# A two-block hybrid network on one core: linear-attention decays laid out by key and query, five early up/gate tiles, first loads on two queues

## The chip, the cores and the metric

The kernel runs on one NeuronCore of a Trainium2 chip as one launch. The metric is device time in microseconds, the median of several executions. Lower is better. The engines that matter here are TensorE (PE; PEld is its weight load), VectorE (DVE), ScalarE (ACT), GpSimd (POOL) and SyncE (SP), which issues the loads.

## The reference

The input is x with 256 tokens of width 1024. Two networks run one after the other, each with two layers. A layer is a feed-forward stage, a mixer, and a second feed-forward stage; so there are eight feed-forward stages and four mixers.

```
def hybrid_layer(x, ...):                       # first network, twice
    x = x + 0.5 * swiglu(rmsnorm(x, ffn1_norm), wg, wu, wd)      # 1024 -> 2816 -> 1024
    h = rmsnorm(x, mix_norm); proj = h @ w_in
    na_o  = rmsnorm(neighbourhood_attention(na_q, na_k, na_v, rpb), na_gain)     # 8 heads of 64
    o_fwd = gla_chunked(qg, kg, vg, log_gf, True)                # 4 heads, dk 64, dv 128
    o_bwd = flip(gla_chunked(flip(qg), flip(kg), flip(vg), flip(log_gb), False))
    gla_o = rmsnorm(o_fwd + o_bwd, gla_gain) * silu(g_r)
    x = x + concat([na_o, gla_o]) @ w_out
    return x + 0.5 * swiglu(rmsnorm(x, ffn2_norm), ...)

def gla_chunked(q, k, v, g, include_diag):      # gated linear attention, one direction
    b = cumsum(g)
    a[t, s] = sum_d q[t, d] * k[s, d] * exp(b[t, d] - b[s, d])   # s <= t, or s < t
    o[t] = sum_s a[t, s] * v[s]                 # the state between chunks continues the same sum
```

The second network's feed-forward stages are the same with a shift, a scale and a gate that come from a vector c (modulation: c times nine matrices of 1024 x 1024 a layer); its mixers are a recurrent unit with block attention, and a sparse attention.

## The kernel before

**Layout.** x lies transposed in SBUF, as eight tiles of 128 features by 256 tokens (`k.x`). A matmul takes a 128x128 block of weights as the stationary operand and 256 tokens as the moving one. All weights are fp32; each is split into a high part (`wh`, fp32r, made on ScalarE, L319) and the rest (`wl`, made on VectorE, L332), and so are the activations.

**The weight stream** (`Stream`, L257 to L362). The weights are a list of chunks of 1 MB, 16 blocks of 128x128 each. A chunk is loaded on SyncE's queue into `stg` (L308), split, and used by TensorE in order. `AHEAD` chunks are split before TensorE uses them. Among the chunks of the first feed-forward stages stand pieces of the modulation matrices, which VectorE multiplies with c and sums (L701).

**The start** (`begin`, L271). The first chunk and x come in four pieces each; both were issued in turn on SyncE's queue (L283, L284). ScalarE and VectorE split each piece as it lands, and the first matmuls follow.

**A feed-forward stage** (`ffn`). It has 22 up/gate tiles. A tile is one chunk: eight blocks for gate, eight for up, 256 tokens, into one PSUM tile (`pp`, two of them). The RMS norm is not waited for. Tiles below `OLD` (0, 1 and 2) use the split of the unnormalised x times the norm's gain (`Hh`, `Hl`) with three matmuls a block (`mm3`, L622 to L624: wh Hh, wh Hl, wl Hh), and the row factor `rs` is multiplied in afterwards (L750). Here this is called the early form. During tile 1 the row factor is made (`norm_sum`, `norm_spread`), and then a background generator, `renorm` (L577), makes the normalised and split H, eight feature tiles one by one: a product on VectorE or GpSimd (L584), a copy to fp32r on ScalarE, the rest on VectorE (L687 without a shift, L684 with one). Tiles from `OLD` on read H with two matmuls a block (`mm2`, L606 of 512 columns, that is low and high part of H side by side, and L607 of 256). Then the down projection (`pd`) follows from `act`.

**Background work.** `tick()` is called after every few blocks of a tile; each call advances every generator in `self.bg` by one step, to its next `yield`. What a step issues is queued on the engines behind what was issued before; on TensorE the order is the order of issue. In a feed-forward tile there are four steps, in a q/k tile of mix1 two, in the last value projection of mix1 one after each 128 rows of weights.

**mix1** (two stages, at about 204 to 335 us and 704 to 840 us). Generators run beside the projections: `na_pair` for each pair of attention heads, and `gla_grams`, then `gla_out`, for the linear attention. `gla_grams` builds the 256 x 256 matrix a (keys by queries) for four heads and both directions in levels: blocks of 8, then pairs of half-blocks of 8, 16, 32 and 64, then the two halves of 128. INC is the running sum of the log gates, VAL the same shifted for the backward direction. For a level, `dist` makes the differences to the block's middle on VectorE (L941, L942) and their exponential on ScalarE (L943); `weigh` multiplies with q or k (L947, L948); `gram` is eight products on TensorE (16 matmul instructions, fp32, 64 partitions each, L955) into two PSUM tiles; `place` copies them under a mask into `at` (L965). The first index of the tensors was the direction, so each level had a Gram group for each direction. The order is one step `weigh`, one step the forward group, and so on, set by the `yield`s and `wait`s.

Of the kernel before, what the change touches and what calls it, by code (L numbers as in the profile page):

```python
# [17 lines left out]
P = 128  # L18
# [97 lines left out]
def gla_masks():  # L116

    s, t = np.arange(P)[:, None], np.arange(P)[None]
    m = [(s // 8 == t // 8) & (s > t)]
    for h in LEVELS:  # L120
        same = s // (2 * h) == t // (2 * h)
        left, right = s % (2 * h) < h, t % (2 * h) >= h
        m += [same & left & right, same & ~left & ~right]
    return np.ascontiguousarray(np.stack(m, 1).astype(np.uint8)).reshape(P, -1).view(np.int32)


# [130 lines left out]
class Stream:  # L257
# [13 lines left out]
    def begin(self, x, start, split):  # L271

        k, nc = self.k, self.k.nc
        t = k.wp.tile([P, CH * P], F32, name="stg", tag="stg")
        h = k.hp.tile([P, CH * P], F32R, name="wh", tag="wh", bufs=self.AHEAD + 2)
        l = k.hp.tile([P, CH * P], F32R, name="wl", tag="wl")
        parts = [slice(a, b) for a, b in PIECES]

        def part(w, m):
            return w.rearrange("p (g k n) -> p g k n", g=2, n=P)[:, :, m]  # L280

        for m in parts:
            nc.sync.dma_start(k.x[:, m], x[:, m])  # L283
            nc.sync.dma_start(part(t, m), part(self.plan[0][1], m))  # L284
        nc.sync.dma_start(k.ident, k.a["ident"])
        self.loaded = 1
        start()
        for m in parts:
            split(m.start)
            nc.scalar.activation(part(h, m), part(t, m), AF.Copy)  # L290
            nc.vector.tensor_sub(part(l, m), part(t, m), f(part(h, m)))
            for i in range(m.start + 1, m.stop):
                split(i)
        self.high = self.ready = 1
        self.parts[0] = (h, l)
        self.split_hi()
        self.prep()
# [68 lines left out]
SUM_ONE = 0, 7  # L366
SUM_TWO = 1, 7

OLD = 3

PIECES = (0, 2), (2, 4), (4, 6), (6, 8)

# [6 lines left out]
class Kern:  # L379
    def __init__(self, ctx, nc, tc, a, o):  # L380
        self.ctx, self.nc, self.tc, self.a, self.o = ctx, nc, tc, a, o
        self.wp = ctx.enter_context(tc.tile_pool(name="wp", bufs=Stream.LOADS))
        self.hp = ctx.enter_context(tc.tile_pool(name="hp", bufs=Stream.AHEAD + 1))
        self.cp = ctx.enter_context(tc.tile_pool(name="cp", bufs=1))
        self.tp = ctx.enter_context(tc.tile_pool(name="tp", bufs=2))
        self.pd = ctx.enter_context(tc.tile_pool(name="pd", bufs=2, space=PSUM))
        cp, nc = self.cp, self.nc
        self.x = cp.tile([P, KD, S], F32, name="x")
        self.Hh = cp.tile([P, KD, S + 2], F32R, name="Hh")
        self.Hl = cp.tile([P, KD, S], F32R, name="Hl")  # L390
# [6 lines left out]
        nc.scalar.activation(self.mhalf, self.ones[:, :8], AF.Copy, scale=-0.5)  # L397
# [179 lines left out]
    def renorm(self, pool, tp):  # L577
# [4 lines left out]
        for i in range(KD):  # L582
            y = tp.tile([P, S], F32, name="y", tag="y", bufs=3)
            (nc.gpsimd if i % 2 else nc.vector).tensor_tensor(y, x[:, i], rs, op=OP.mult)  # L584
            lo, hi = self.H[:, i, 0], self.H[:, i, 1]
            if shift is None:
                self.split(hi, lo, y, g[:, i:i + 1])
            else:
                h = tp.tile([P, S], F32, name="h", tag="h", bufs=2)
                nc.scalar.activation(h, y, AF.Identity, scale=g[:, i:i + 1], bias=shift[:, i:i + 1])  # L590
                self.split(hi, lo, h)
            if i % 2:
                yield
# [202 lines left out]
    def mix1(self, st, l, then):  # L796
        nc = self.nc
        with self.tc.tile_pool(name="mx", bufs=1) as mp, self.tc.tile_pool(name="m2", bufs=2) as m2, \
# [5 lines left out]
            wgate = mp.tile([64, S], F32, name="wgate")  # L804
            nc.gpsimd.memset(code, 1.0)
            nc.sync.dma_start(wgate, self.a[f"wgate_{l}"])
            qkq = mp.tile([P, 3, 2, S], F32, name="qkq")
            vg = mp.tile([P, 2, 512], F32, name="vg")
            vn = mp.tile([P, 2, 512], F32, name="vn")
            self.na = mp.tile([P, 4, S], F32, name="na")  # L810
# [21 lines left out]
                self.small()  # L832
            for i in range(2):
                p = self.tiles(st)
                nc.vector.scalar_tensor_tensor(qkq[:, 0, i], p[:, 0], 0.125, self.rs, op0=OP.mult, op1=OP.mult)
                nc.vector.tensor_mul(qkq[:, 1, i], p[:, 1], self.rs)
                nc.scalar.activation(qkq[:, 2, i], qkq[:, 0, i], AF.Copy)
            while gates in self.bg:
                self.tick()
            at = self.mp.tile([P, GH, 4, P], F32, name="at")  # L840

            def gla():
                yield from self.gla_grams(qkq, at)
                yield
                yield from self.gla_out(l, at, vg, sgr)

# [78 lines left out]
    def gla_grams(self, qkq, at):  # L925
        nc, mp, m2 = self.nc, self.mp, self.m2
        packed = mp.tile([P, (1 + 2 * len(LEVELS)) * P // 4], mybir.dt.int32, name="masks")
# [7 lines left out]
        def ref(h):  # L935
            r = INC.rearrange("p a i (n two h) -> p (a i n) two h", two=2, h=h)[:, :, 0, h - 1:h]
            return r.to_broadcast([P, 1024 // (2 * h), h])
# [12 lines left out]
        def gram(ks, qs, d, so=(0, P), to=(0, P)):  # L950

            ps = [self.pd.tile([P, 2, 2, P], F32, name="pg", tag="pd") for _ in range(2)]
            for i, j, hh in [(i, j, hh) for i in range(2) for j in range(2) for hh in range(2)]:
                r = slice(64 * hh, 64 * hh + 64)
                nc.tensor.matmul(ps[hh][:, i, j], ks[r, d[j], i, so[j]:so[j] + P], qs[r, d[j], i, to[j]:to[j] + P],  # L955
                                 start=True, stop=True)
            return ps

        def place(ps, m):
# [6 lines left out]


        d8 = m2.tile([P, 2, 2, S], F32, name="d8", tag="E")
        XR = mp.tile([P, 2, 2, S], F32, name="XR", tag="az")
        XL = mp.tile([P, 2, 2, S], F32, name="XL", tag="G")  # L970
# [6 lines left out]
        nc.vector.tensor_mul(XR, XR, qkq[:, 0:2])  # L977
        nc.vector.tensor_mul(XL, XL, qkq[:, 1:3])
        yield from wait(3)
        weigh(E, LEVELS[0])  # L980
        todo = (gram(XL, XR, (0, 0)), None)
        yield from wait(2)
        place(*todo)
        todo = (gram(XR, XL, (1, 1)), 0)
        yield from wait(2)
        hs = LEVELS + (128,)
        for n, h in enumerate(LEVELS):
            nxt = hs[n + 1]
            place(*todo)
            E2 = dist(nxt)  # L990
            todo = (gram(E, E, (0, 0)), 1 + 2 * n)
            yield from wait(2)
            place(*todo)
            weigh(E2, nxt)
            todo = (gram(E, E, (1, 1)), 2 + 2 * n)
            E = E2
            yield from wait(2 if n < 2 else 1)
        place(*todo)
        todo = gram(E, E, (0, 1), (0, P), (P, 0))
# [685 lines left out]
```

## Time and profile before

| | |
|---|---|
| median of 3 runs | 2029.94 us (2028.47 to 2030.31) |
| the profiled execution | 2029.0 us, span 2027.2 us |
| mean granted TensorE clock | 0.995 |
| PE busy | 1980.2 us, 98% |
| DVE busy | 1608.9 us, 79% |
| ACT busy | 1188.2 us, 59% |
| HBM read | 427.86 MB, 212 GB/s over the span |

The profile is one execution. Times in it count from the first instruction. An engine's busy share is an average over stages; what a stage waits for is read from the idle time ahead of its instructions and from what ended it (behind the arrow). A clock of 1.00 is 2.4 GHz, 0.50 is 1.2 GHz.

### The profile page before, as it was taken

The page shows a single profiled execution, that of the slowest core. Times are in us where ns is not written, and L with a number is a line of the kernel's source. Part 1 is how long each engine was busy: PE and PEld are TensorE (multiplying, and loading weights), DVE is VectorE, ACT ScalarE, POOL GpSimd, SP SyncE. Part 2 cuts the span into 40 slices and gives each one's busy share as a digit, 9 for nine tenths or more (in the row PEclk, how much of TensorE's full clock was granted, in tenths as well). Part 3 has the DMA queues.
Part 4 walks back from the last instruction along what each step waited for, and adds up shares of the span by engine and source line. Part 5 has one row for each costly group of instructions (what it writes and reads, how often), then busy time and mean ns, then how long its engine had stood idle before and what let it go on. Part 6 is the DMA issues. An engine that isn't in the chain of part 4 may idle for free.

```text
span 2027.2 us, 32869 instructions
## 1 busy us (share of the span) xinstructions
PE 1980.2 (98%) x13012; PEld 1778.4 (88%) x13012; DVE 1608.9 (79%) x2562; ACT 1188.2 (59%) x1990; POOL 181.0 (9%) x200
## 2 busy tenths in 40 slices
PE   7999999999999999999999999999999999999998
PEld 6888989888888898988888889888898888878887
DVE  8886797987888689798878877898667667978663
ACT  6654656554555465665555547575546555877552
POOL 2001002000100100200120010120010001101001
PEclk9999999999999999999999999999999999999999
DMA  7776434877588643487758765358555556315551
GB/s 283 292 282 247 164 143 157 292 271 288 211 287 294 234 158 140 157 307 275 268 184 293 284 246 185 125 218 290 188 189 185 187 189 201 121 43 188 189 188 60
DMA packets 67882, 431.03 MB, mean 213 GB/s; under 512 B 11408, under 2 KB 14096, under 8 KB 16656
## 3 DMA queue, kind: packets, MB, share of 16 engines
q1 hardware_dynamic: 67728, 428.94, 58.8%
q8 instruction: 102, 1.67, 0.3%
q14 instruction: 52, 0.43, 0.1%
HBM read 427.86 MB, written 1.05 MB: 212 GB/s over the span
## 4 chain that ended last, share of the span: by engine, by line
PE 82%; DVE 10%; ACT 4%; DMA 2%; issue 1%; POOL 0%; SPq 0%; DVEq 0%; ACTq 0%; POOLq 0%
PE pp L606 27%; PE pd L606 16%; PE pp L607 14%; PE pd L607 8%; DVE wl L332 3%; PE pp L622 2%; PE pp L623 2%; PE pp L624 2%; PE po L885 2%; ACT wh L319 1%; PE pt L1277 1%; PE pg L955 1%; DVE t L750 1%; DVE H L687 1%; PE pv L672 1%
## 5 line engine op out<-in xcount | busy, mean ns | idle before, releaser
L332 DVE TENSOR_TENSOR wl<-stg,wh 128x1024 fp32r<-128x1024 f32 x646 | 788.3, 1247 | 124.9 <-PE pp L607 57.3
L606 PE MATMUL pp<-H,wh 128*128 128x512 f32 x2432 | 849.6, 392 | 15.8 <-DVE H L687 7.9
L319 ACT ACTIVATE wh<-stg 128x1024 fp32r<-128x1024 f32 x646 | 668.3, 1053 | 327.2 <-PE pp L606 145.8
L607 PE MATMUL pp<-H,wl 128*128 128x256 f32 x2432 | 686.9, 283 | 0.0
L606 PEld LDWEIGHTS pp<-H,wh 128*128 128x128 f32 x2432 | 458.3, 189 | 115.7 <-DVE H L687 9.5
L606 PE MATMUL pd<-act,wh 128*128 128x512 f32 x1408 | 488.5, 390 | 0.0
L607 PEld LDWEIGHTS pp<-H,wl 128*128 128x128 f32 x2432 | 461.6, 190 | 0.3
L607 PE MATMUL pd<-act,wl 128*128 128x256 f32 x1408 | 397.1, 282 | 0.0
L606 PEld LDWEIGHTS pd<-act,wh 128*128 128x128 f32 x1408 | 264.3, 188 | 55.4
L622 PE MATMUL pp<-Hh,wh 128*128 128x258 f32 (+1 forms) x936 | 271.9, 291 | 7.0 <-ACT wh L290 6.3
L624 PE MATMUL pp<-Hh,wl 128*128 128x258 f32 (+1 forms) x936 | 264.7, 283 | 2.1 <-DVE wl L332 1.2
L607 PEld LDWEIGHTS pd<-act,wl 128*128 128x128 f32 x1408 | 266.1, 189 | 0.0
L623 PE MATMUL pp<-Hl,wh 128*128 128x256 f32 x936 | 264.2, 282 | 1.9 <-DVE Hl L687 1.9
L701 DVE SCALAR_TENSOR_TENSOR stg<-stg,cond 128x1024 f32<-128x1024 f32 x144 | 175.7, 1222 | 29.8 <-DMA stg<-mw 27.3
L622 PEld LDWEIGHTS pp<-Hh,wh 128*128 128x128 f32 x936 | 177.2, 189 | 11.8 <-ACT wh L290 6.3
L623 PEld LDWEIGHTS pp<-Hl,wh 128*128 128x128 f32 x936 | 178.4, 191 | 3.7 <-DVE Hl L687 2.5
L624 PEld LDWEIGHTS pp<-Hh,wl 128*128 128x128 f32 x936 | 177.4, 190 | 3.0 <-DVE wl L332 1.6
L683 ACT ACTIVATE act<-a 128x256 fp32r<-128x256 f32 x176 | 73.3, 417 | 128.5 <-DVE a L759 126.3
L522 POOL TENSOR_TENSOR acc<-sq 128x256 f32<-128x256 f32 x16 | 17.8, 1113 | 1204.5 <-ACT sq L518 1129.6
L684 DVE TENSOR_TENSOR act<-a,act 128x256 fp32r<-128x256 f32 x176 | 76.4, 434 | 45.9 <-ACT act L683 45.9
L522 POOL TENSOR_TENSOR acc<-acc,sq 128x256 f32<-128x256 f32 x87 | 78.6, 906 | 333.8 <-ACT sq L518 329.6
L615 DVE TENSOR_TENSOR t<-pp,c 128x512 f32<-128x512 f32 x152 | 104.0, 684 | 2.4 <-ACT c L613 2.4
(316 smaller groups left out, 2086.0 us busy)
## 6 DMA issues: line engine op xcount, KB each, us to landing
stg<-b SPq DMA_DIRECT2D x132, 1024.0 KB, 4.8
stg<-a SPq DMA_DIRECT2D x129, 1024.0 KB, 4.8
stg<-mw SPq DMA_DIRECT2D x72, 1024.0 KB, 5.2
stg<-m SPq DMA_DIRECT2D x34, 1024.0 KB, 4.8
stg<-m2a SPq DMA_DIRECT2D x14, 1024.0 KB, 4.8
stg<-m2b SPq DMA_DIRECT2D x12, 1024.0 KB, 4.8
stg<-nab SPq DMA_DIRECT2D x4, 1024.0 KB, 4.7
cond<-cond SPq DMA_DIRECT2D x6, 512.0 KB, 4.0
```

The source lines that it names most:

```text
L319: self.k.nc.scalar.activation(h[:, sl], self.raw[c][:, sl], AF.Copy)
L332: self.k.nc.vector.tensor_sub(l[:, sl], t[:, sl], f(h[:, sl]))
L522: nc.gpsimd.tensor_tensor(s2, acc, sq, op=OP.add)
L606: mm(p, h, parts, start=start, stop=False)
L607: return mm(p[:, :S], l, parts[:, 1], start=False, stop=stop)
L615: self.nc.vector.tensor_tensor(t, p[:, :, S:], c, op=OP.add)
L622: mm(out[:, :n], h, self.Hh[:, kt, :n], start=start and clear, stop=False, skip_group_check=not clear)
L623: mm(out[:, :S], h, self.Hl[:, kt], start=False, stop=False, skip_group_check=not clear)
L624: return mm(out[:, :n], l, self.Hh[:, kt, :n], start=False, stop=stop, skip_group_check=not clear)
L683: nc.scalar.activation(hi, src, AF.Copy)
L684: nc.vector.tensor_sub(lo, src, f(hi))
L701: self.nc.vector.scalar_tensor_tensor(sl, sl, 1.0, self.cond, op0=OP.mult, op1=OP.mult, accum_out=self.mod[l][:, 2 * c + g:2 * c + g + 1])
```

## The change

Four edits in one. `gla_grams` lays the decayed tensors out by key (0) and query (1) in place of direction; in a level the left half of a block belongs to the forward direction for keys and to the backward one for queries, so one Gram group and one mask give both. Its waits are set anew: three steps a level. `OLD` goes from 3 to 5, and `renorm` yields after each feature tile in place of every second. The first two x pieces are issued on ScalarE's queue, and the small constant `mhalf` is made behind them. `na_pair` takes the PSUM tile of a head and issues both products of this head before the next head's.

```
 def gla_masks():
-        m += [same & left & right, same & ~left & ~right]
+        m.append(same & (left == right))
 def begin():
-        for m in parts:
-            nc.sync.dma_start(k.x[:, m], x[:, m])
+        for n, m in enumerate(parts):
+            (nc.scalar if n < 2 else nc.sync).dma_start(k.x[:, m], x[:, m])
             nc.sync.dma_start(part(t, m), part(self.plan[0][1], m))
+        nc.scalar.activation(k.mhalf, k.ones[:, :8], AF.Copy, scale=-0.5)      # was in __init__
-OLD = 3
+OLD = 5
 def renorm():
-            if i % 2:
-                yield
+            yield
 def mix1():
-            qkq = mp.tile([P, 3, 2, S], F32, name="qkq")
+            kq = mp.tile([P, 2, 2, S], F32, name="kq")
-                nc.vector.scalar_tensor_tensor(qkq[:, 0, i], p[:, 0], 0.125, self.rs, op0=OP.mult, op1=OP.mult)
-                nc.vector.tensor_mul(qkq[:, 1, i], p[:, 1], self.rs)
-                nc.scalar.activation(qkq[:, 2, i], qkq[:, 0, i], AF.Copy)
+                nc.vector.scalar_tensor_tensor(kq[:, 1, i], p[:, 0], 0.125, self.rs, op0=OP.mult, op1=OP.mult)
+                nc.vector.tensor_mul(kq[:, 0, i], p[:, 1], self.rs)
 def gla_grams():
         def dist(h):
-            nc.vector.tensor_sub(cut(E, h, 1), cut(VAL, h, 1), ref(h))
-            nc.vector.tensor_sub(cut(E, h, 0), ref(h), cut(VAL, h, 0))
+            for d in range(2):
+                nc.vector.tensor_sub(cut(E[:, 1 - d:2 - d], h, 1), cut(VAL[:, d:d + 1], h, 1), ref(INC[:, d:d + 1], h))
+            nc.vector.tensor_sub(cut(E, h, 0), ref(INC, h), cut(VAL, h, 0))
             nc.scalar.activation(E, E, AF.Exp, scale=1.0 / 16)
-        def weigh(E, h):
-            nc.vector.tensor_mul(cut(E, h, 1), cut(E, h, 1), cut(qkq[:, 0:2], h, 1))
-            nc.vector.tensor_mul(cut(E, h, 0), cut(E, h, 0), cut(qkq[:, 1:3], h, 0))
+        def weigh(E):
+            nc.vector.tensor_mul(E, E, kq)
...
-        nc.scalar.activation(XR, d8, AF.Exp, scale=1.0 / 16)
-        nc.scalar.activation(XL, d8, AF.Exp, scale=-1.0 / 16)
+        for d in range(2):
+            for a in range(2):
+                nc.scalar.activation(X[d][:, a], d8[:, d], AF.Exp, scale=(-1.0 if a == d else 1.0) / 16)
...
-        for n, h in enumerate(LEVELS):
-            nxt = hs[n + 1]
+        for n in range(len(LEVELS)):
             place(*todo)
-            E2 = dist(nxt)
-            todo = (gram(E, E, (0, 0)), 1 + 2 * n)
+            E2 = dist(hs[n + 1])
+            todo = (gram(E[:, 0], E[:, 1]), 1 + n)
             yield from wait(2)
-            place(*todo)
-            weigh(E2, nxt)
-            todo = (gram(E, E, (1, 1)), 2 + 2 * n)
+            weigh(E2)
             E = E2
-            yield from wait(2 if n < 2 else 1)
+            yield
 def na_pair():
-        ss = [self.ps.tile([P, 2, S], F32, name="pss", tag="st", bufs=self.nst) for _ in range(2)]
-        for qt in range(2):
-            for hh, p in enumerate(ss):
-                r = slice(64 * hh, 64 * hh + 64)
+        ss = []
+        for hh in range(2):
+            r = slice(64 * hh, 64 * hh + 64)
+            p = self.ps.tile([P, 2, S], F32, name="pss", tag="st", bufs=self.nst)
+            for qt in range(2):
                 nc.tensor.matmul(p[:, qt], qk[r, 0, qt * P:(qt + 1) * P], qk[r, 1], start=True, stop=True)
+            ss.append(p)
```

## Rows read from the trace of the kernel before

**Rows 1.** The page, part 1: busy us, share of the span, instructions.

```profile
PE 1980.2 (98%) x13012; PEld 1778.4 (88%) x13012; DVE 1608.9 (79%) x2562; ACT 1188.2 (59%) x1990; POOL 181.0 (9%) x200
```

**Rows 2.** Groups by line and form: busy us, mean ns, idle us before, releasers.

```profile
L606 PE MATMUL pp<-H,wh 128*128 128x512 f32 x2432 | 849.6, 392 | 15.8 <-DVE H L687 7.9 <-DVE H L684 6.3 <-DVE b L693 1.7
```

**Rows 3.** Stretches of tile 3, line 606: length, busy (count), clock, DMA; eight summed.

```profile
29.01:41.58 12.57, 8.39 (x17) 4.26 (x17) 0.73 0.55 204
...
1047.09:1058.27 11.18, 7.35 (x16) 3.72 (x17) 0.85 0.26 95
...
sum 67.79, PE 50.40 PEld 25.92; mean PE 6.30 PEld 3.24
```

**Rows 4.** Stretches of tile 8, line 606: the sum of eight stages.

```profile
sum 44.39, PE 44.39 PEld 24.04; mean PE 5.55 PEld 3.00
```

**Rows 5.** Stretches: PE, PEld, DVE, ACT, POOL busy, granted clock, DMA share, GB/s.

```profile
33.83:40.66 6.83, 5.97 (x18) 5.09 (x19) 6.83 (x14) 3.90 (x7) 0.90 (x1) 0.50 0.49 170
279.59:283.00 3.41, 3.41 (x13) 2.59 (x14) 3.41 (x6) 0.79 (x2) 0.00 (x0) 0.50 0.00 0
1054.41:1057.83 3.42, 3.42 (x13) 2.84 (x12) 2.87 (x4) 0.42 (x1) 0.00 (x0) 0.50 0.00 0
```

**Rows 6.** Stretches of tile 2, line 622: the first and the sum of eight.

```profile
23.36:29.01 5.65, 4.47 (x16) 2.89 (x16) 1.00 0.70 271
...
sum 45.53, PE 36.00 PEld 23.13; mean PE 4.50 PEld 2.89
```

**Rows 7.** A stretch, columns as in rows 5, while tile 3 of the first stage waits.

```profile
30.00:36.00 6.00, 2.16 (x8) 1.41 (x7) 6.00 (x11) 3.65 (x7) 1.99 (x2) 0.82 0.71 276
```

**Rows 8.** Timeline of DVE, first feed-forward stage: start us, us, instruction.

```profile
36.03 0.47 DVE L687 SCALAR_TENSOR_TENSOR H<-y,cols,H 128x256 fp32r<-128x256 f32 x1
...
39.05 1.21 DVE L332 TENSOR_TENSOR wl<-stg,wh 128x1024 fp32r<-128x1024 f32 x1
...
40.52 1.21 DVE L332 TENSOR_TENSOR wl<-stg,wh 128x1024 fp32r<-128x1024 f32 x1
```

**Rows 9.** Groups by line and form, as in rows 2.

```profile
L332 DVE TENSOR_TENSOR wl<-stg,wh 128x1024 fp32r<-128x1024 f32 x646 | 788.3, 1247 | 124.9 <-PE pp L607 57.3 <-PE pd L607 45.2 <-issue 11.6
...
L759 DVE TENSOR_TENSOR a<-s,t 128x256 f32<-128x256 f32 x164 | 69.1, 421 | 32.1 <-ACT s L746 31.7 <-ACT s L753 0.3
...
L965 DVE COPY_PREDICATED at<-masks,pg 128x512 f32<-128x512 uint8 x36 | 24.4, 729 | 2.8 <-PE pg L955 2.8
...
L750 DVE TENSOR_TENSOR t<-pp,rs 128x512 f32<-128x512 f32 x24 | 16.4, 683 | 7.5 <-ACT rs L569 6.5 <-PE pp L624 0.9
...
L943 ACT ACTIVATE E<-E 128x1024 f32<-128x1024 f32 x10 | 10.5, 1052 | 10.6 <-DVE E L942 10.6
```

**Rows 10.** Timeline of PE in the first mix1: start us, us, instruction.

```profile
269.45 1.13 PE L1057 MATMUL pss<-qk 64*128 64x256 f32 x8
...
274.24 1.16 PE L955 MATMUL pg<-E 64*128 64x128 f32 x16
275.33 1.08 PE L1091 MATMUL pav<-pt,vn 128*64 128x256 f32 x8
...
277.86 0.67 PE L1057 MATMUL pss<-qk 64*128 64x256 f32 x2 [0.42 <-DVE qk L856]
279.47 1.99 PE L1057 MATMUL pss<-qk 64*128 64x256 f32 x6 [0.95 <-ACT sq L518]
...
304.91 1.89 PE L1017 MATMUL pgo<-at,vg 128*128 128x256 f32 x8
```

**Rows 11.** Timeline of SP, the first and the last issue of x.

```profile
1.18 0.42 SPq L283 DMA_DIRECT2D x<-xT  x1
...
4.84 0.60 SPq L283 DMA_DIRECT2D x<-xT  x1
```

**Rows 12.** The chain that ended last, the first tile: start us, us, what.

```profile
4.84 5.72 DMA x<-xT
```

**Rows 13.** A stretch, columns as in rows 5: the first pieces land.

```profile
6.30:13.20 6.90, 5.94 (x25) 5.51 (x26) 6.90 (x10) 5.11 (x11) 4.49 (x6) 1.00 0.97 340
```

More of the change, by code (lines that the diff above doesn't have):

```diff
@@ L396, in __init__ @@
         nc.gpsimd.memset(self.ones, 1.0)
-        nc.scalar.activation(self.mhalf, self.ones[:, :8], AF.Copy, scale=-0.5)
         nc.sync.dma_start(self.cols[:, :KD], a["cols"][:, :KD])
@@ L842, in gla @@
             def gla():
-                yield from self.gla_grams(qkq, at)
+                yield from self.gla_grams(kq, at)
                 yield
@@ L923, in gla_gates, with gla_grams @@
         nc.scalar.activation(self.VAL[:, 0], self.INC[:, 0], AF.Copy)
-    def gla_grams(self, qkq, at):
+    def gla_grams(self, kq, at):
         nc, mp, m2 = self.nc, self.mp, self.m2
-        packed = mp.tile([P, (1 + 2 * len(LEVELS)) * P // 4], mybir.dt.int32, name="masks")
+        packed = mp.tile([P, (1 + len(LEVELS)) * P // 4], mybir.dt.int32, name="masks")
         nc.sync.dma_start(packed, self.a["masks"])
@@ L933, in cut, with ref, gram @@
             return t.rearrange("p a i (n two h) -> p (a i n) two h", two=2, h=h)[:, :, half]
-        def ref(h):
-            r = INC.rearrange("p a i (n two h) -> p (a i n) two h", two=2, h=h)[:, :, 0, h - 1:h]
-            return r.to_broadcast([P, 1024 // (2 * h), h])
+        def ref(t, h):
+            r = cut(t, h, 0)[:, :, h - 1:h]
+            return r.to_broadcast([P, r.shape[1], h])
         def dist(h):
             E = m2.tile([P, 2, 2, S], F32, name="E", tag="E")
-            nc.vector.tensor_sub(cut(E, h, 1), cut(VAL, h, 1), ref(h))
-            nc.vector.tensor_sub(cut(E, h, 0), ref(h), cut(VAL, h, 0))
+            for d in range(2):
+                nc.vector.tensor_sub(cut(E[:, 1 - d:2 - d], h, 1), cut(VAL[:, d:d + 1], h, 1), ref(INC[:, d:d + 1], h))
+            nc.vector.tensor_sub(cut(E, h, 0), ref(INC, h), cut(VAL, h, 0))
             nc.scalar.activation(E, E, AF.Exp, scale=1.0 / 16)
             return E
-        def weigh(E, h):
-            nc.vector.tensor_mul(cut(E, h, 1), cut(E, h, 1), cut(qkq[:, 0:2], h, 1))
-            nc.vector.tensor_mul(cut(E, h, 0), cut(E, h, 0), cut(qkq[:, 1:3], h, 0))
-        def gram(ks, qs, d, so=(0, P), to=(0, P)):
+        def weigh(E):
+            nc.vector.tensor_mul(E, E, kq)
+        def gram(ks, qs, so=(0, P), to=(0, P)):
             ps = [self.pd.tile([P, 2, 2, P], F32, name="pg", tag="pd") for _ in range(2)]
@@ L954, in gram @@
                 r = slice(64 * hh, 64 * hh + 64)
-                nc.tensor.matmul(ps[hh][:, i, j], ks[r, d[j], i, so[j]:so[j] + P], qs[r, d[j], i, to[j]:to[j] + P],
-                                 start=True, stop=True)
+                nc.tensor.matmul(ps[hh][:, i, j], ks[r, i, so[j]:so[j] + P], qs[r, i, to[j]:to[j] + P], start=True, stop=True)
             return ps
@@ L968, in gla_grams @@
         d8 = m2.tile([P, 2, 2, S], F32, name="d8", tag="E")
-        XR = mp.tile([P, 2, 2, S], F32, name="XR", tag="az")
-        XL = mp.tile([P, 2, 2, S], F32, name="XL", tag="G")
+        X = [mp.tile([P, 2, 2, S], F32, name=f"X{d}", tag=tag) for d, tag in enumerate(("az", "G"))]
         v8 = [t.rearrange("p a i (n e) -> p (a i n) e", e=8) for t in (VAL, INC, d8)]
         nc.vector.tensor_sub(v8[2], v8[0], v8[1][:, :, 3:4].to_broadcast([P, P, 8]))
-        nc.scalar.activation(XR, d8, AF.Exp, scale=1.0 / 16)
-        nc.scalar.activation(XL, d8, AF.Exp, scale=-1.0 / 16)
+        for d in range(2):
+            for a in range(2):
+                nc.scalar.activation(X[d][:, a], d8[:, d], AF.Exp, scale=(-1.0 if a == d else 1.0) / 16)
         yield
         E = dist(LEVELS[0])
-        nc.vector.tensor_mul(XR, XR, qkq[:, 0:2])
-        nc.vector.tensor_mul(XL, XL, qkq[:, 1:3])
+        for x in X:
+            nc.vector.tensor_mul(x, x, kq)
         yield from wait(3)
-        weigh(E, LEVELS[0])
-        todo = (gram(XL, XR, (0, 0)), None)
+        weigh(E)
+        todo = (gram(X[0][:, 0], X[0][:, 1]), None)
         yield from wait(2)
         place(*todo)
-        todo = (gram(XR, XL, (1, 1)), 0)
+        todo = (gram(X[1][:, 0], X[1][:, 1]), 0)
         yield from wait(2)
         hs = LEVELS + (128,)
-        for n, h in enumerate(LEVELS):
-            nxt = hs[n + 1]
+        for n in range(len(LEVELS)):
             place(*todo)
-            E2 = dist(nxt)
-            todo = (gram(E, E, (0, 0)), 1 + 2 * n)
+            E2 = dist(hs[n + 1])
+            todo = (gram(E[:, 0], E[:, 1]), 1 + n)
             yield from wait(2)
-            place(*todo)
-            weigh(E2, nxt)
-            todo = (gram(E, E, (1, 1)), 2 + 2 * n)
+            weigh(E2)
             E = E2
-            yield from wait(2 if n < 2 else 1)
+            yield
         place(*todo)
-        todo = gram(E, E, (0, 1), (0, P), (P, 0))
+        todo = gram(E[:, 0], E[:, 1], (0, P), (P, 0))
         yield from wait(2)
```

## The prediction

> **What bounds the kernel now.** I read the page first. TensorE is busy 98% of the span and VectorE 79% [rows 1]. Matmuls are pipelined, so a busy TensorE need not be at its peak; I therefore went on to the idle column of the grouped instructions, to the stretches of single tiles, and to the waits in the TensorE timeline. The reader is to see that weights stream in ahead and TensorE sets the end almost everywhere, and that its largest waits have one place. The first matmul that reads the renormalised H idled 15.8 us in all, 14.2 of it behind VectorE's H instructions [rows 2].
>
> That place is tile 3 of the 22 up/gate tiles of each of the eight feed-forward stages (tiles counted from 0). The eight tiles 3 take 67.79 us together [rows 3]; eight steady tiles take 44.39, or 5.55 us each [rows 4]. The difference is 23.4 us: 7.0 in the first stage, 5.6 in the fifth, 1.1 to 2.7 in the other six. Part of it is clock: after the two long waits the granted clock was 0.50 for 6.83 and 3.42 us, the 1.2 GHz level instead of 2.4 [rows 5], which costs (6.83 + 3.42) / 2 = 5.1 us of the 23.4. Two more stages matter: the two mix1 stages, where the Gram groups stand in the TensorE queue, and the first 17 us.
>
> **Five early tiles (OLD 3 to 5).** Tiles 3 and 4 leave the H form (two matmuls a block, 512 and 256 columns) for the early form (three of about 256). A tile of the early form took 45.53 / 8 = 5.69 us, 5.65 in the first stage [rows 6]. Two such tiles in eight stages cost 16 x (5.69 - 5.55) = 2.3 us. The first use of H moves back by two tiles, 11.4 us. The whole wait per stage was at most 7.0 us, so the H wait ends before tile 5 everywhere if VectorE does the same work at the same pace.
>
> What is late next is VectorE itself: it is busy 6.00 of 6 us while tile 3 of the first stage waits [rows 7]. The last H there ended at 36.50, and the weights of tile 5 (wl) at 41.73 [rows 8]. Without the wait, tile 5 starts at 29.01 + 2 x 5.65 = 40.3. The list of VectorE work up to that wl is the same as before, plus one more product t of 0.68 us [rows 9]. So the first half of that wl comes at 39.05 + 1.21 + 0.68 = 40.9 and the second at 42.4, while TensorE wants them at 40.3 and, half a tile later, at 43.1. I charge 0.7 us there and 0.5 for the other stages: residue 1.2 us. The finer yields of renorm (eight steps instead of four) order this work, and add none; they spread it until the middle of tile 3, and leave one and a half tiles of cover. Upper bound of the residue: half of all 23.4 comes back at tile 5, 11.7 us. Lower bound: none. Net of this edit: 23.4 - 2.3 - 1.2 = 19.9 us less.
>
> **One Gram group a level.** A layer had eleven groups of 16 matmul instructions: two for the blocks of 8, eight for the four levels, one across the halves. It will have seven. A group takes 275.33 - 274.24 = 1.09 us of TensorE until the next work starts [rows 10]. Eight groups less over two layers are 8.7 us; I add 0.3 for a group of the second layer that stalled on the placing of its predecessor. The number of passages between Gram and projection work stays about the same, because the new groups fall on their own steps (every third) where the old shared theirs with the attention pairs. On VectorE a level loses one pair of masked copies (2 x 0.73) and gains 0.16 in dist (two half-size differences of some 0.42 in place of one of 0.68); weigh becomes one product of 128x1024, for which the nearest row is wl at 1.25, against 2 x 0.68 [rows 9]. That is 1.4 us a level less on VectorE, which is beside TensorE's work; I cost it at nothing. On ScalarE the copies of q go and four half-size exponentials replace two whole ones, under a microsecond, also beside.
>
> The wait it adds: a level's group now follows its own weigh by one step, and the chain of a level is in series: two masked copies 1.5, dist 1.5, exponential 1.05, weigh 1.25, together 5.3 us [rows 9]. Behind a waiting group in TensorE's queue stand the value projection and the attention pairs. Between two groups there are three steps. In the q/k tiles that is half a tile a step, 8.5 us of cover; in the last value projection a step is about 0.7 us of projection, and attention work of 1.0 to 2.1 us is on most steps. I take no stall; bounds 0 and 1 us for each of eight levels.
>
> **Scores of a pair, half by half (na_pair).** Before, the four score products alternated between the heads on partitions 0 to 63 and 64 to 127. The row shows eight instructions of 256 columns done in 1.13 us, while eight full-height ones of 256 columns, strictly one after the other, took 1.89 us [rows 10]: a step is 0.216 us, and alternating halves ran two at a time. In the new order both products of one head come first. Nothing in the trace has that order. If the queue starts in program order, the second head's first product can overlap only with the last of the first head: seven steps instead of four, 3 x 0.216 = 0.65 us more. The fourth pair of each layer had a wait in the middle (0.95 us for the second head's bank [rows 10]); there the first head's second product fills the wait and I charge nothing. Six pairs x 0.65 = 3.9 us. Bounds: 0 if the halves still run together, 8 x 0.76 = 6.1 us if nothing overlaps. The Trainium skill, "TensorE: Matmul & The Clock Gate", Part 3, states that matmuls keep program order strictly and that only weight loads of another row group are pulled ahead. By that rule the 3.9 stands; without it the two streams might drift past each other, and the sum below would come to 2000.2.
>
> Mix1 together: 9.0 - 3.9 = 5.1 us less.
>
> **First loads on two queues.** The four x pieces alternate with the weight pieces in SyncE's list, and the chain that ends the first tile runs through the last x load, issued at 4.84 [rows 11, 12]. Two issues fewer ahead of it are 2 x 0.6 = 1.2 us; the first starts 0.44 sooner (1.18 to 0.74). ScalarE, which issues them now, waits for x in any case, so the two issues hide there together with mhalf behind them (price without that cover: 1.2). But the DMA engines are busy 0.97 of the time while those pieces land [rows 13]. I take 0.8, between 0.4 and 1.2. The Trainium skill, "DMA: Bandwidth & Descriptors", section "Issuing engines are not separate DMA queues", says that all queues share the same 16 engines and that issuing from several saves only the issue time; taken strictly, with engines this full, the gain would be 0.4 and the sum 0.4 us longer.
>
> **Sum.** 19.9 + 5.1 + 0.8 = 25.8 us off the profiled execution's own 2029.0 (span 2027.2): 2003.2. The median shown is 0.94 above that execution, so 2004.
>
> **Rivals.**
> (a) VectorE is the bound of the early tiles, and the wait only moves to tile 5. For it: 6.00 of 6 us busy [rows 7]. Against: the six smaller stages waited 1.1 to 2.7 us and get 11.4 us more. Half of 23.4 stays: 2029.94 - 25.8 + 10.5 (11.7 less the 1.2 already charged) = 2015.
> (b) The score products still overlap, or their price falls into waits that pairs had anyway (0.42 and 0.95 us in one pair [rows 10]), and the 3.41 us at the low clock behind those waits [rows 5] do not come again. 2004 - 3.9 - 1.7 = 1998.
> (c) Slower: the level chain in series is exposed. Each level's Gram group then stands in TensorE's queue until masked copies, dist, exponential and weigh are through, 5.3 us, eight levels, 42 us: 2046. It decides from 25.8 / 8 = 3.2 us of exposure a level. Against: the steps hold 4 to 10 us of TensorE work on all but the last.
> (d) The early tiles do not do what they say: H's instructions stay behind the weights' in VectorE's queue, and the whole wait comes two tiles later. Then only mix1 and the start count, 2029.94 + 2.3 - 5.9 = 2026.
>
> **Chances.** Forecast 0.58 (its own range 1999 to 2009), (a) 0.15, (b) 0.18, (c) 0.04, (d) 0.05. The range for eight in ten takes in most of (a) and (b): 1996 to 2014. A difference of 0.2% (4 us) is about what a measurement of this kernel can tell from none. Faster: 0.92, from the forecast, (a), (b) and a part of (d); same 0.04, the rest of (d) and a mild (c); slower 0.04.
>
> **What the profile after would show.** Tile 5 of each feed-forward stage at 5.6 to 6.5 us and no H wait above 1 us; no clock of 0.50 near 34 and 1054; tiles 3 and 4 at 5.6 to 5.8. If tile 5 takes over 7 us in several stages, (a) is right. In mix1 seven Gram groups a layer of about 1.1 us; a group that idles over 2 us behind E speaks for (c). Score products of a pair over 1.13 + 0.65 us show the lost overlap, near 1.13 show (b). The first matmul at 5.9 instead of 6.29. The prediction is wrong if the up/gate halves as a whole lose less than 12 us or more than 24, or mix1 grows.

## The result and the profile after

The changed kernel takes 2002.51 us (median of 4 runs, 2000.78 to 2003.83). The kernel before took 2029.2 beside it: a ratio of 0.9869, 95% interval 0.9852 to 0.9886. The forecast was 2004.0, so the total came out 1.5 us lower. By terms it did not come out so well; one term was right in size for a reason that is wrong.

The page's first part of the kernel after, as in [rows 1]:

```profile
PE 1966.3 (98%) x13140; PEld 1779.5 (89%) x13140; DVE 1592.5 (80%) x2554; ACT 1180.5 (59%) x1974; POOL 186.4 (9%) x200
```

Groups by line and form, as in [rows 2, 9]: the first matmul that reads H, weigh, and the Gram products of the levels.

```profile
L605 PE MATMUL pp<-H,wh 128*128 128x512 f32 x2176 | 755.1, 390 | 0.6 <-DVE t L614 0.6
...
L948 DVE TENSOR_TENSOR E<-E,kq 128x1024 f32<-128x1024 f32 x10 | 12.2, 1220 | 4.6 <-ACT E L944 4.6
L955 PE MATMUL pg<-E 64*128 64x128 f32 x160 | 11.7, 286 | 0.0
```

The 15.8 us for which TensorE sat idle ahead of H are 0.6. No Gram product waits.

Stretches of tile 3 (line 621) and then of tile 5 (line 605) of the eight feed-forward stages, the first, the fifth and the sum; columns as in [rows 3, 4]:

```profile
28.29:33.94 5.65, 4.47 (x17) 3.01 (x17) 1.00 0.81 307
...
1030.69:1036.42 5.73, 4.52 (x16) 2.99 (x17) 1.00 0.42 173
...
sum 45.55, PE 35.99 PEld 24.03; mean PE 4.50 PEld 3.00
```

```profile
39.59:45.19 5.60, 5.59 (x16) 3.01 (x17) 1.00 0.71 255
...
1042.15:1047.70 5.55, 5.55 (x16) 3.00 (x17) 1.00 0.86 311
...
sum 44.50, PE 44.48 PEld 24.02; mean PE 5.56 PEld 3.00
```

Tile 3 is a plain tile now (67.79 to 45.55 for eight), and the wait has not moved to tile 5. Of the three stretches at half clock [rows 5], two are gone:

```profile
33.83:40.66 6.83, 6.83 (x57) 6.65 (x56) 6.83 (x13) 5.31 (x10) 0.93 (x1) 1.00 0.46 163
280.81:284.22 3.41, 3.41 (x17) 3.13 (x18) 2.71 (x4) 3.11 (x5) 0.00 (x0) 0.50 0.19 29
```

By stage, from the first matmul of a stage to that of the next, the profiled executions (spans 2027.2 and 2001.0) differ so: the up/gate halves of the eight feed-forward stages together from 1026.24 to 1005.75 (20.5 less), from the end of up/gate to the next stage's start over the two mix1 from 193.90 and 192.92 to 191.18 and 189.96 (5.7 less), the other mixers and the down projections within 0.3.

In mix1 stand the scores (pss), one Gram group, the fourth pair's scores, and a wait that was not there before. Timeline of TensorE, as in [rows 10]:

```profile
253.26 1.14 PE L1054 MATMUL pss<-qk 64*128 64x256 f32 x8 [0.42 <-DVE qk L854]
...
265.42 1.16 PE L955 MATMUL pg<-E 64*128 64x128 f32 x16
...
269.83 1.45 PE L1054 MATMUL pss<-qk 64*128 64x256 f32 x8 [0.30 <-DVE su L1071]
...
279.37 1.57 PE L1089 MATMUL pav<-pt,vn 128*64 128x256 f32 x8 [1.92 <-ACT pt L1082]
...
779.78 1.57 PE L1089 MATMUL pav<-pt,vn 128*64 128x256 f32 x8 [1.96 <-ACT pt L1082]
```

The scores took 1.14 us in the new order, as the 1.13 in the old one. The attention values (pav) idled 1.92 us for the copy of pt, and 1.96 at the same place of the second layer; behind the first the clock fell to 0.50. What holds the copy up is seen one and two engines back. VectorE's timeline there, and then ScalarE's:

```profile
273.34 0.68 DVE L1061 TENSOR_TENSOR e<-pss,stg 128x512 f32<-128x512 f32 x1
274.06 0.69 DVE L1063 TENSOR_REDUCE mx<-e 128x2 f32<-128x512 f32 x1
274.66 0.68 DVE L1061 TENSOR_TENSOR e<-pss,stg 128x512 f32<-128x512 f32 x1
275.26 1.22 DVE L948 TENSOR_TENSOR E<-E,kq 128x1024 f32<-128x1024 f32 x1
276.39 0.68 DVE L1063 TENSOR_REDUCE mx<-e 128x2 f32<-128x512 f32 x1
```

```profile
277.10 0.51 ACT L1066 ACTIVATE e<-e,mx 128x256 f32<-128x256 f32 x1 [1.22 <-DVE mx L1063]
...
278.72 1.08 ACT L1082 ACTIVATE pt<-pt 128x512 f32<-128x512 f32 x2
```

A weigh of 1.22 us stands between the second head's sum e and its maximum mx. ScalarE idles 1.22 us for that maximum, and the copy of pt is queued on ScalarE behind these exponentials although it does not need them. VectorE's list is not in the order of the source here: in the source nothing stands between the two heads' sums and maxima. So the sentence on background work ahead, that a step is queued on the engines behind what was issued before, does not hold for VectorE.

### The profile page after: what moved, and what is told of

Read it like the earlier page. It is cut to its first block, busy times and chain, and to the rows that moved or that the text cites. A ratio compares the mean times of both kernels' runs of the same rounds, so it can differ in the third digit from the quotient of the medians.

```text
span 2001.0 us, 33084 instructions
## 1 busy us (share of the span) xinstructions
PE 1966.3 (98%) x13140; PEld 1779.5 (89%) x13140; DVE 1592.5 (80%) x2554; ACT 1180.5 (59%) x1974; POOL 186.4 (9%) x200
## 4 chain that ended last, share of the span: by engine, by line
PE 85%; DVE 8%; DMA 3%; ACT 2%; issue 1%; POOL 1%; DVEq 0%; SPq 0%; ACTq 0%; POOLq 0%
PE pp L605 23%; PE pd L605 16%; PE pp L606 12%; PE pd L606 8%; PE pp L621 5%; PE pp L623 5%; PE pp L622 5%; DVE wl L333 3%; PE po L883 2%; DMA stg<-mw 1%; ACT wh L320 1%; PE pt L1275 1%; DVE Hl L686 1%; PE pv L671 1%; PE pv L672 1%
## 5 line engine op out<-in xcount | busy, mean ns | idle before, releaser
L605 PE MATMUL pp<-H,wh 128*128 128x512 f32 x2176 | 755.1, 390 | 0.6 <-DVE t L614 0.6
L606 PE MATMUL pp<-H,wl 128*128 128x256 f32 x2176 | 613.6, 282 | 0.0
L605 PEld LDWEIGHTS pp<-H,wh 128*128 128x128 f32 x2176 | 408.4, 188 | 86.5 <-DVE t L614 1.2
L606 PEld LDWEIGHTS pp<-H,wl 128*128 128x128 f32 x2176 | 411.2, 189 | 0.1
L621 PE MATMUL pp<-Hh,wh 128*128 128x256 f32 (+1 forms) x1192 | 343.5, 288 | 7.0 <-ACT wh L291 6.5
L622 PE MATMUL pp<-Hl,wh 128*128 128x256 f32 x1192 | 335.4, 281 | 1.8 <-DVE Hl L686 1.8
L623 PE MATMUL pp<-Hh,wl 128*128 128x256 f32 (+1 forms) x1192 | 336.5, 282 | 0.5 <-DVE wl L333 0.4
L621 PEld LDWEIGHTS pp<-Hh,wh 128*128 128x128 f32 x1192 | 225.0, 189 | 11.6 <-ACT wh L291 6.5
L622 PEld LDWEIGHTS pp<-Hl,wh 128*128 128x128 f32 x1192 | 226.5, 190 | 3.7 <-DVE Hl L686 2.4
L745 ACT ACTIVATE s<-t 128x256 f32<-128x256 f32 x136 | 56.6, 416 | 78.6 <-DVE t L614 78.4
```

The source lines that it names most:

```text
L605: mm(p, h, parts, start=start, stop=False)
L606: return mm(p[:, :S], l, parts[:, 1], start=False, stop=stop)
L621: mm(out[:, :n], h, self.Hh[:, kt, :n], start=start and clear, stop=False, skip_group_check=not clear)
L622: mm(out[:, :S], h, self.Hl[:, kt], start=False, stop=False, skip_group_check=not clear)
L623: return mm(out[:, :n], l, self.Hh[:, kt, :n], start=False, stop=stop, skip_group_check=not clear)
L745: nc.scalar.activation(s, t[:, 0], AF.Silu)
```

## The experiments

**Each part alone, on the kernel before.** Five early tiles with the eight yields of renorm:

```
-OLD = 3
+OLD = 5
-            if i % 2:
-                yield
+            yield
```

> The kernel before with the five early tiles and the eight yields of renorm alone. The prediction's step: 19.9 us less, with up to 1.2 us of wait left at tile 5. Theory now (from the trace after): the up/gate parts carry 19 to 21 us of the whole, the eight tiles 5 stand at 5.55 to 5.60 each, and the low clock near 34 and 1054 is gone. Rival (only the whole change as a whole gives it, as earlier stages shift when H is due): under 16 us.

Measured: 2010.04 us against 2028.93 (ratio 0.9906, 0.9893 to 0.9920), 18.9 less; the up/gate halves sum to 1004.83, 21.4 less, tiles 5 to 44.47, and the low clock near 34 and 1054 is gone. The step stands on its own.

The Gram change alone (masks, `kq`, `gla_grams` as in the change; all else as before):

> The kernel before with the one Gram group a level alone (masks, layout by key and query, gla_grams); scores and early tiles as before. The prediction's step: 9.0 us less. Theory now: the four groups saved a layer are 4.4 us a layer, of which 1.9 us comes back as a wait of the attention values (pav) on the copy of pt, so 5 to 6 us less in all. Rival: that wait comes from the new order of the scores, then it is absent here and the change is 8 to 9 us less.

Measured: 2019.38 (0.9956, 0.9943 to 0.9968), 9.6 less; the two mix1 stretches are 188.58 and 188.62, 5.3 and 4.3 less. The wait at pav is 1.06 us here, not 1.9. So the theory that the Gram change itself brings the 1.9 falls, and the rival stands. Neither mix1 stage of this trace has a stretch at half clock, as the kernel before has one in its first [rows 5]; measured against the second stage before, which has none either, a stage is 4.3 us shorter, 8.6 for two.

The order of the scores alone (`na_pair` as in the change):

> The kernel before with the scores of a pair half by half alone. The prediction's step: 3.9 us more (six pairs, 0.65 us each, as the queue starts in program order). Theory now: the two 64-row halves run side by side also in this order, eight instructions in 1.05 to 1.15 us; 0 us, within 0.5. If the order only saves the wait for the second bank, up to 1.9 us less.

Measured: 2028.9 (0.9995, 0.9986 to 1.0004), no difference. Its scores on TensorE's timeline:

```profile
253.91 1.14 PE L1058 MATMUL pss<-qk 64*128 64x256 f32 x8 [0.28 <-DVE qk L856]
```

Eight instructions in 1.14 us, both halves of the rows side by side. The 0.65 us a pair of the prediction is not there. That TensorE's list is in the new order shows in the starts: the two halves start 13 ns apart here, and 6 ns apart where they alternate in the kernel before.

The first loads alone (`begin` and `mhalf` as in the change):

> The kernel before with the first two x loads on ScalarE's queue and mhalf behind them alone. The prediction's step: 0.8 us less (0.4 to 1.2), first matmul at 5.9. Theory now: the first matmul is not earlier (6.4 to 6.5), but tile 2 starts 0.7 us earlier, 22.6 to 22.7 instead of 23.36. Rival: that gain came with the early tiles, not with the loads, and tile 2 starts at 23.3 to 23.4.

Measured: 2026.6 (0.9990, 0.9981 to 0.9999), 2.3 less with an interval of 0.2 to 3.9. The first matmul starts at 6.66, later than before; tile 2 starts at 22.62 in place of 23.36, 0.74 earlier. The stage shows 0.7; the rest of the 2.3 is not accounted for. In the nine traces with the new loads tile 2 starts at 22.6 to 23.5, in the four with the old ones at 23.2 and 23.4, and at 25.2 and 25.1 in e2 and e3, where the clock was 0.50 for 3.41 us from 17.91 and 17.53. No trace with the new loads has that stretch. How often the kernel before has it is not known.

The parts alone sum to 30.8 us, the whole gives 26.4 against the same 2028.93. Some 4 us are lost between them. The intervals of the five times together are wider than that; the stages say it more firmly, as the two mix1 stages sum to 377.2 us in e2 and to 381.1 in the changed kernel.

**Where the 4 us go.** The changed kernel with the old order of the scores:

```
-        ss = []
-        for hh in range(2):
...
+        ss = [self.ps.tile(...) for _ in range(2)]
+        for qt in range(2):
+            for hh, p in enumerate(ss):
```

> The changed kernel with the scores of a pair alternating between the heads again. The parts alone gave 18.9, 9.6, 0.0 and 2.3 us, 30.8 together, the whole change 26.4: 4.4 us are lost between them. Theory: the new order of the scores costs them. With it VectorE's list has the weigh of the level of 16 between the two maxima (mx) of pair 3, so pair 3's exponentials and the copy of pt behind them on ScalarE come 1 us later, and the attention values wait 1.92 us instead of 1.06; qk comes later too, and the clock falls to 0.50 near 280. Undone: 3.5 to 5 us less than the changed kernel (1997.5 to 1999), no stretch at 0.50 near 280, wait of pav about 1.1. Rival: the early tiles or the start shift mix1; then 0 us (2001 to 2004).

Measured: 1998.45 (1998.26 to 1999.14; ratio 0.9854, 0.9839 to 0.9868). That is 4.1 us below the changed kernel's median and 3.0 by the two ratios; the two mix1 stages are 2.6 and 1.2 shorter, the first of them without its stretch at half clock. In VectorE's list the two maxima stand together again. The attention values, and the stretches around:

```profile
278.58 1.57 PE L1087 MATMUL pav<-pt,vn 128*64 128x256 f32 x8 [1.05 <-ACT pt L1080]
```

```profile
270.00:280.00 10.00, 8.95 (x72) 6.79 (x72) 10.00 (x24) 6.86 (x18) 0.73 (x1) 1.00 0.30 106
280.00:284.00 4.00, 4.00 (x39) 3.52 (x40) 2.98 (x4) 3.51 (x6) 0.98 (x1) 1.00 0.20 37
```

So the new order of the scores costs nothing in the kernel before (e3) and 3 to 4 us beside the new Gram steps. This version beats both kernels. It does not yet say whether TensorE's order or VectorE's list is the cause. The next one leaves the scores half by half and moves only the weigh:

```
-            weigh(E2)
+            if n == 2:
+                with self.tc.issue_after(self.mx):      # self.mx: the last maximum
+                    weigh(E2)
+            else:
+                weigh(E2)
...
```

> The changed kernel, scores half by half as in it, with one edge of order more: the weigh before the level of 64 is queued on VectorE behind the second maximum (mx) of pair 3. VectorE's list is otherwise the same but for one masked copy. Theory: that weigh between the two maxima is what the new order of the scores costs at the attention values. Moved: pav waits 1.0 to 1.2 us in place of 1.92, no clock of 0.50 near 280; 1.8 to 3.5 us less than the changed kernel (1999 to 2000.7); what is left to e5_alternate are the waits of the score products for qk (0.64 and 0.82 us). Rival: it is the order of the products themselves on TensorE; then pav still waits 1.9 us and the time stays at 2001 to 2004.

Measured: 2000.5 (0.9863, 0.9847 to 0.9880), 2.0 below the changed kernel by the medians and 1.2 by the two ratios, whose intervals overlap. VectorE, then TensorE:

```profile
273.88 0.69 DVE L1067 TENSOR_REDUCE mx<-e 128x2 f32<-128x512 f32 x1
274.48 0.68 DVE L1065 TENSOR_TENSOR e<-pss,stg 128x512 f32<-128x512 f32 x1
275.19 0.69 DVE L1067 TENSOR_REDUCE mx<-e 128x2 f32<-128x512 f32 x1
...
275.87 1.21 DVE L948 TENSOR_TENSOR E<-E,kq 128x1024 f32<-128x1024 f32 x1
```

```profile
278.18 1.56 PE L1093 MATMUL pav<-pt,vn 128*64 128x256 f32 x8 [0.92 <-ACT pt L1086]
```

The wait falls from 1.92 to 0.92 (1.96 to 0.95 in the second layer), no stretch near 280 is at 0.50, and the scores are still half by half. The place of that weigh is the cause of this wait. (It is the weigh of the level of 8: the loop runs 64, 32, 16, 8. The two expectations name it wrongly.) The time alone (2000.5 between 1999 and 2002.5) would not settle it; the rows do. But the wait is not the whole loss. The two mix1 stages are 1.8 and 0.5 us shorter than in the changed kernel, where e5 gave 2.6 and 1.2: 2.2 of 3.8 us, most of them in the stage that lost its stretch at half clock. What is left to e5, 0.8 us a layer, was not taken apart further. Here the scores of the second pair wait 0.32 and 0.65 us for qk, there not, and VectorE's list differs at that place too: a masked copy stands ahead of qk here, behind it there. In e5 the third pair waits longer instead, and TensorE's waits in the two stages sum to 4.3 us in both. The last Gram group of a layer takes 0.4 us longer here than there.

**How far one half of the rows runs ahead.** The changed kernel, the Gram products head half by head half:

```
-            for i, j, hh in [(i, j, hh) for i in range(2) for j in range(2) for hh in range(2)]:
+            for i, j, hh in [(i, j, hh) for hh in range(2) for i in range(2) for j in range(2)]:
```

> The changed kernel with the eight products of a Gram group issued head half by head half: four products on rows 0 to 63, then four on rows 64 to 127. 14 groups. Prediction's rule (starts in program order): only the seam overlaps, 15 steps of 0.11 us in place of 8, 0.8 us a group, 11 us more. Rival (each half of the rows runs its own queue as far as instructions are at hand): a group stays at 1.1 to 1.3 us, 0 to 3 us more. If the look-ahead covers only a part, a group of 1.4 to 1.7 us.

And on e5_alternate, in twos (`for i ... for hh ... for j`):

> e5_alternate with the products of a Gram group issued in twos: two products (four instructions) on rows 0 to 63, then two on rows 64 to 127, then again. In e6 the second half of the rows began with the fifth instruction of the first, so four instructions of it were taken ahead. If that is the reach, two products and two products run fully side by side, as the scores do: a group of 1.09 to 1.2 us. If starts kept to program order but for the seams: 13 steps of 0.11, 1.65 us.

One level's group in e6, and then in e10:

```profile
265.83 1.71 PE L955 MATMUL pg<-E 64*128 64x128 f32 x16
```

```profile
266.20 1.26 PE L955 MATMUL pg<-E 64*128 64x128 f32 x16
```

From first start to the next work's start that is 1.64 and 1.19 us, against 1.09 in the changed kernel: neither of the two ends, but the case between. In e6 the first instruction of the second half starts 6 ns after the fifth of the first half, before the sixth to eighth, which stand ahead of it in the program; with four and four (e10, and the scores) both halves start together. So starts are not in program order across the two halves, and the reach was three instructions that were passed. The Trainium skill, "TensorE: Matmul & The Clock Gate", Part 3, has matmuls start strictly in program order; here the measurement differs, and it decides.

The times: e6 2003.83 (0.9880, 0.9865 to 0.9895), 1.3 above the changed kernel by the medians and 2.2 by the ratios, although its Gram groups are busy 7.6 us more. Its scores wait 0.0 us in all in place of 2.1, pav 1.0 and 1.3 in place of 1.9 and 2.0, and the clock does not fall near 280: part of the longer groups stands where TensorE would have waited. The rest was not taken apart. e10 2001.31 (0.9862, 0.9842 to 0.9881; two runs); 1.6 of its distance of 2.9 to e5 stand in tiles 1 and 2 of the fifth stage, see below.

**The yields, and one early tile less.** The changed kernel with renorm yielding after every second tile, and with `OLD = 4`:

> The changed kernel with renorm yielding after every second feature tile, as before. The prediction's step: the finer yields order the work and add none; within 1 us, tile 5 at 5.55 to 5.6. Rival: they keep H's work from piling up ahead of the weights on VectorE; then tiles 2 to 4 of the first and fifth stage wait for weights, 2 us or more in all.

> The changed kernel with four early tiles in place of five. A tile in the early form costs 0.10 to 0.18 us more than with H, so 8 x 0.14 = 1.1 us less where H is ready a tile earlier; H was late by 1.1 to 7.0 us at tile 3, so at tile 4 the first and the fifth stage should still wait 1.4 us or less, the other six not. Expected: 1 us less to 1 us more. Rival: VectorE is the bound of the first stage's early tiles, and the wait comes back at tile 4 there with the clock at 0.50: 3 us or more above the changed kernel.

Measured: e7 2005.08 (0.9886, 0.9871 to 0.9901), e8 2005.18 (0.9884, 0.9868 to 0.9901), 2.6 and 2.7 above the changed kernel by the medians, 3.4 and 3.0 by the ratios, with intervals that still touch the changed kernel's. In e7 tile 3 of the first stage takes 7.27 us, as t stands behind three H instructions on VectorE. TensorE, then VectorE:

```profile
35.77 0.36 PE L622 MATMUL pp<-Hh,wh 128*128 128x256 f32 x1 [1.46 <-DVE t L750]
```

```profile
33.29 1.74 DVE L687 SCALAR_TENSOR_TENSOR H<-y,cols,H 128x256 fp32r<-128x256 f32 x3
34.95 0.68 DVE L750 TENSOR_TENSOR t<-pp,rs 128x512 f32<-128x512 f32 x1
```

1.6 us of the 2.6 are this; 1.2 more stand in tiles 1 and 2 of the fifth stage, where the clock was 0.50 for 3.41 us from 1025.99. In e8 six of the eight tiles 4 stand at 5.55 and the sixth stage's at 6.14, but that of the first takes 10.7 us; I had expected 1.4 us of wait there at most. TensorE, then VectorE:

```profile
38.76 0.47 PE L605 MATMUL pp<-H,wh 128*128 128x512 f32 x1 [2.54 <-DVE t L749]
...
39.80 0.45 PE L606 MATMUL pp<-H,wl 128*128 128x256 f32 x1 [0.57 <-DVE wl L333]
```

```profile
34.42 1.77 DVE L700 SCALAR_TENSOR_TENSOR stg<-stg,cond 128x1024 f32<-128x1024 f32 x1
...
36.12 1.22 DVE L700 SCALAR_TENSOR_TENSOR stg<-stg,cond 128x1024 f32<-128x1024 f32 x1
...
37.94 0.68 DVE L749 TENSOR_TENSOR t<-pp,rs 128x512 f32<-128x512 f32 x1
```

VectorE is behind there (two modulation products of 1.77 and 1.22 us ahead of t), and the mean clock from 40 to 44 was 0.58. So rival (a)'s mechanism exists: VectorE is the bound of the first stage's early tiles, and the fifth early tile is just what it takes. With five, in the changed kernel, the last H of that stage ends 1.25 us after tile 5 has begun (39.59), and no wait follows:

```profile
39.97 0.87 DVE L686 SCALAR_TENSOR_TENSOR H<-y,cols,H 128x256 fp32r<-128x256 f32 x2
```

**The fifth stage's tile 1.** It grew from 8.51 to 9.94 us with the change, and in other kernels here it is anything from 8.4 to 10.7. In this tile the norm waits on VectorE for two modulation products, and these for c. The load of c and its Silu, in the kernel before and then in the changed one (SyncE and ScalarE each):

```profile
1027.31 0.33 SPq L767 DMA_DIRECT2D cond<-cond  x1
1031.28 1.06 ACT L777 ACTIVATE cond<-cond 128x1024 f32<-128x1024 f32 x1 [0.82 <-DMA cond<-cond]
```

```profile
1009.48 0.33 SPq L766 DMA_DIRECT2D cond<-cond  x1
1014.87 1.06 ACT L776 ACTIVATE cond<-cond 128x1024 f32<-128x1024 f32 x1 [2.23 <-DMA cond<-cond]
```

From issue to Silu that is 3.97 and 5.39 us: the 1.4 us by which the tile grew. It is 3.9 to 4.1 in e2, e3, e4 and e8 (three or four early tiles), 4.5 in e1 and 5.1 to 5.4 in the six others with five early tiles that load c anew. Why the load lands later there is not known. The tiles over 10 us, in e6, e7 and e10, have a stretch of 3.41 us at half clock besides, from 1023.98, 1025.99 and 1021.08. e5_alternate with c kept in SBUF across two adjoining feed-forward stages:

```
-            if cond_needed:
-                self.cond = ap.tile([P, D], F32, name="cond")
+            if fresh:                                  # first of two adjoining stages only
                 nc.sync.dma_start(self.cond, self.a["cond"])
...
```

> e5_alternate, and c (cond) is kept in SBUF from the second feed-forward stage of a layer to the first of the next, where the two follow each other, in place of a new load and a new Silu at the start of the next. Theory: the 9.7 us of tile 1 of the fifth stage come from that load (5.3 us from issue to use, then Silu and two modulation products of 1.22 us ahead of the norm on VectorE; TensorE waits 2.4 us for rc). Held: tile 1 of the fifth stage at 6.4 to 7.5 us, the whole 2 to 3.5 us below e5_alternate (1995 to 1996.5). Rival: the modulation products themselves, or the load of the matrix (stg from mw), hold the norm up; then tile 1 stays above 9 and the time within 1 us of 1998.5.

Rows of the changed kernel first (VectorE and TensorE), then of e5 and of e9 (TensorE):

```profile
1015.96 1.23 DVE L700 SCALAR_TENSOR_TENSOR stg<-stg,cond 128x1024 f32<-128x1024 f32 x1 [2.57 <-ACT cond L776]
```

```profile
1022.83 0.41 PE L544 MATMUL pbc<-ident,rc 128*128 128x128 f32 x2 [2.71 <-DVE rc L557]
```

```profile
1019.25 0.40 PE L544 MATMUL pbc<-ident,rc 128*128 128x128 f32 x2 [2.44 <-DVE rc L557]
```

```profile
1017.47 0.40 PE L545 MATMUL pbc<-ident,rc 128*128 128x128 f32 x2 [1.50 <-DVE rc L558]
```

Measured: 1998.98 (0.9852, 0.9836 to 0.9869), not to be told from e5's 1998.45; tile 1 at 8.73 in place of e5's 9.67. The load costs 0.9 us of it, as the wait for rc falls from 2.44 to 1.50. The other 1.5 are there with c at hand: the two modulation products still stand ahead of the norm's arithmetic on VectorE. My 2 to 3.5 us were too much, and the time itself shows no gain.

## Why the prediction was right or wrong

**Early tiles: right, with one cost too many and one too few.** Predicted 19.9 less; 18.9 by the time of e1, 20.5 in the up/gate halves of the changed kernel, of which 0.9 lie in tiles 0 and 1 of the first stage and belong to the start. The 23.4 went, tiles in the early form cost 5.65 and 5.73 as charged, and the low clock went. The residue at tile 5 was 0.1 us and not 1.2. In its place 1.4 us came at tile 1 of the fifth stage (the load of c) and 1.1 from tile 12 of the sixth on (a load of a modulation piece came late; no other kernel here has it at that place), neither of which I looked for. The step "the finer yields order this work, and add none", costed at nothing, was wrong: without them tile 3 of the first stage waits (e7), 1.6 us.

**Gram groups: right.** Predicted 9.0 less, 9.6 alone (e2), or 8.6 without what the clock gave. The chain of a level in series was not exposed: no Gram group waits, and rival (c) had nothing to show.

**Scores: the step that failed.** "If the queue starts in program order, the second head's first product can overlap only with the last of the first head": it overlapped from its first instruction. Eight instructions took 1.14 us in e3 and in the changed kernel. That is what rival (b) said of the scores. The sentence "Nothing in the trace has that order" was wrong as well. `gla_gates` of the kernel before issues two products on partitions 0 to 31 and then two on 32 to 63 (32 rows each, not 64), eight instructions of 256 columns, and they took 1.14 us side by side:

```profile
218.92 1.14 PE L905 MATMUL zp<-code,wgate 32*128 32x256 f32 x8
```

That row, and not a rule, should have set the term at nothing. The 3.9 us charged are nevertheless near what was lost (3 to 4 us, e5), and that is luck, as the mechanism is another: for 2.2 of 3.8 us (e11) VectorE's list put a weigh between two maxima, and ScalarE's queue carried that to TensorE; the other 1.6 stay open. With this term right, the sum would have been 2000, and the kernel was 2002.5. The second half of rival (b), the low clock in mix1 gone, did not hold: behind the new wait it came back at 280.81.

**Start: right in size.** Predicted 0.8, found 0.7 at tile 2. The stated sign was wrong: the first matmul came at 6.46, not at 5.9, and at 6.2 to 6.7 in all nine kernels with the new loads (6.1 to 6.3 in the four with the old). What the earlier loads took away were the waits of tiles 0 and 1 for wl (0.96 and 0.73 us before, 0.39 after), and 0.47 came back as a wait for POOL:

```profile
6.46 0.58 PE L621 MATMUL pp<-Hh,wh 128*128 128x256 f32 x1 [6.46 <-ACT wh L291]
15.48 0.38 PE L623 MATMUL pp<-Hh,wl 128*128 128x256 f32 x1 [0.39 <-DVE wl L333]
17.74 0.61 PE L529 MATMUL pst<-ones,acc 128*128 128x1 f32 x4 [0.47 <-POOL acc L522]
```

## What to carry to other kernels

Where a wait of a few us recurs in many stages, its length against the cover of one more early tile gave the gain within a twentieth here; but a last tile of cover may be exactly enough, so take it out again once as a test. An edit that reorders products on one engine is to be priced by what it does to the lists of the others: an instruction of 1.2 us that slips between two short ones reached TensorE over two queues. Parts that are measured alone and do not add up point to such a place. And before a term is taken from a rule, it is worth looking whether the trace has the same pattern under another name, as the gate products had here.

## What was not expected of the hardware

Products on partitions 0 to 63 and on 64 to 127 ran side by side also when issued one half after the other, as long as no more than three instructions had to be passed: 1.14 us for four and four instructions of 256 columns, 1.19 for groups of four and four of 128 columns twice, 1.64 for eight and eight (1.09 when they alternate).

A wait of 1.92 us in the first mix1 was followed by 3.41 us at the 1.2 GHz level; one of 1.96 us at the same place of the second layer by none (the stretch 780 to 784 stands at 1.00). In e4, whose mix1 is that of the kernel before, the fall came in the second layer and not in the first. Over all traces, four of the six mix1 stages with a pav wait of 1.9 us (the changed kernel, e7, e8) had such a stretch, and none of the twelve with 0.9 to 1.3 (e2, e5, e6, e9, e10, e11). Where one of a kernel's two mix1 stages had it, that stage was 0.9 to 1.7 us longer than the other. A wait of 1.9 us thus may cost that much more than itself, or nothing.
